# A hybrid decoder trunk on one core: the two parts of a split weight in one shared tile, and the compressed values of both groups in one

## Chip, core and metric

One core of a Trainium2 chip runs the whole program. The metric is device time in microseconds, the median of the runs shown. Engines are named as in the profile: PE (TensorE, matrix products), PEld (its weight loads, which run beside the products), DVE (VectorE), ACT (ScalarE), POOL (GpSimd), SP (SyncE, which issues most transfers).

## What is computed

Two layers of a hybrid decoder over 256 tokens of width 2048. Each layer normalises `x`, applies one wide input projection, feeds its columns to a sparse-attention group and to a Mamba-2 group, and maps the two gated, normalised results back with one output projection:

```python
h = rmsnorm(x, norm_w)
proj = jnp.einsum("bsd,dp->bsp", h, w_in)
(q, kc, vc, ks, vs, kw, vw, gate, z_attn, xbc, dt, z_ssm) = split_columns(proj)
k_cmp = rope(compress_blocks(kc.reshape(kv_shape), pe_k, w1_k, w2_k), pos_cmp)
v_cmp = compress_blocks(vc.reshape(kv_shape), pe_v, w1_v, w2_v)
...
mixed = jnp.concatenate([y_attn, y_ssm], axis=-1)
return x + jnp.einsum("bsm,md->bsd", mixed, w_out)
```

`compress_blocks` makes one compressed key or value for every 16 tokens: chunks of 32 tokens plus a position term, a product with `w1`, SiLU, a product with `w2`. There are two key/value groups.

## The kernel before

**Items.** `ITEMS` (line 55) is a fixed list that one Python loop (line 919) turns into instructions, in an order written out by hand. A "p" item is half a column tile of the input projection, an "o" item a piece of the output projection, a "w" item a piece of the `w1` product. Each layer has 186 p items (93 column tiles, two halves each) and 64 o items. Every p or o item has one weight of 128x1024 floats, loaded by SP into `wr` (five buffers) two to five items ahead.

**Two parts.** To get more precision than one fp32r product gives, each operand is split: `split` (line 154) lets ACT copy the weight into `wh` (the part that fp32r holds) and DVE subtract it from the original into `wl` (the rest). Both have four buffers of 4096 bytes per partition, and both are made two items ahead (`LH = LL = 2`). The other operand is a tile of 512 floats, 256 of one part and 256 of the other.

**A p item** (line 947) has eight pairs: a product of `wh` (stationary, 128 columns) with all 512 columns of the operand tile (moving), and one of `wl` with its first 256 columns. **An o item** (`block`, line 968) has the roles exchanged: 128 columns of the operand tile are stationary, 512 columns of `wh` or `wl` move; 12 products of 512 columns for each item.

**Operand tiles.** In layer 0 the p items move the tiles `h0` to `h15`; the o items of the first half read the Mamba-2 results in `s0` to `s15`, and those of the second half the attention results in `h0` to `h15`. In layer 1 the names are exchanged: p items move `s` tiles, the first half of the o items reads `h`, the second half `s`.

**Addresses.** A tile's place in a partition follows from the order of first allocation and from the sizes, rounded up to 32 bytes; it is software and known before a run. Modulo 256 bytes, the products' operands begin here:

```
                        before
wh, wl (all buffers)    0x80      first ones at 0x19580 and 0x1d580, 4096 bytes apart
h0 to h15               0x80      h0 at 0x21580
s0 to s15               0xc0      s0 at 0x2d6c0
B (att. probabilities)  0x80
V                       0xc0
```

A slice of a tile begins a whole multiple of 512 bytes further, so these numbers hold for every product of a kind.

**Side work.** Small stages are generators in `sides`; `tick` (line 326) advances each by one step at the end of every item, and `W(k)` (line 110) lets a generator rest for `WAITS[k]` items. Each column tile is emptied from PSUM by `evac` (line 341: ACT, DVE), and POOL multiplies it by the norm (`rmul`). For the compression, `build_U` (line 585, three DVE instructions, one call for each of kc 0, kc 1, vc 0, vc 1) adds the position term into `U` after `W(43)`; w items read `U`; `cmp_side` (line 596) applies SiLU into `hd` (line 271, zeroed once at the start by POOL) and the `w2` product. For values (`kv == 1`) eight ACT copies and four DVE subtractions of 32x128 move the result into `VC[0]` and `VC[1]` (lines 629 to 636), which the attention reads at line 796. `v_side` (line 650) transposes a value tile on PE (line 656) into a PSUM tile `t`, of which there are two, copies it with ACT and subtracts with DVE (line 661).

**End of a projection.** In the second half of an output projection DVE adds a finished 128x512 block to `xt`, ACT squares it, and only then come the next copies of `split` in ACT's order (lines 982 to 987).

Of the kernel before, what the change touches and what calls it, by code (L numbers as in the profile page):

```python
# [12 lines left out]
F32R = mybir.dt.float32r  # L13
# [14 lines left out]

NF = 4
WARM = (2, 1, 0, 1, 1, 0, 1, 0)  # L30
WAITS = [1, 0, 0, 4, 0, 2, 0, 0, 0, 2, 0, 2, 0, 0, 0, 1, 1, 2, 0, 0, 0, 1, 1, 0, 3, 3, 2, 2, 0, 2, 1, 1, 2, 1, 0, 1, 1, 1, 1, 4, 3, 1, 1, 3, 4, 0, 1, 0, 0, 4, 4, 2, 2, 0, 1, 2, 0, 2, 2, 0, 1, 1, 1, 3]
EN = 3
ROPE, SINW = 37, 2
W1S, W1N, W1B = 8, 2, 4
# [47 lines left out]
WITEMS = [it for it in ITEMS if it[0] != "w"]  # L82
NS = len(WITEMS)
# [4 lines left out]
def body(ctx: ExitStack, tc: tile.TileContext, wst, w1, xin, xtk, pos, w2, par, con, fin, y):  # L88
    nc = tc.nc
    ACT, DVE, PE, POOL = nc.scalar, nc.vector, nc.tensor, nc.gpsimd  # L90
    HEAD = ((0, 1), (1, 3), (3, 6), (6, 8))
    RS = ((5, 6, 7), (1, 3, 4))
    NR, NH, NL, LH, LL = 5, 4, 4, 2, 2

    pp = ctx.enter_context(tc.tile_pool(name="pp", bufs=1))
    qq = ctx.enter_context(tc.tile_pool(name="qq", bufs=1, space=bass.MemoryType.PSUM))
# [5 lines left out]
    def sb(shape, tag, dt=F32, bufs=1):  # L102
        cnt[0] += 1
        return pp.tile(shape, dt, tag=tag, name=f"{tag}_{cnt[0]}", bufs=bufs)

    def pst(tag, shape=(128, 512), bufs=1):
        cnt[0] += 1
        return qq.tile(list(shape), F32, tag=tag, name=f"p{tag}_{cnt[0]}", bufs=bufs)

    def W(k):  # L110
        for _ in range(WAITS[k]):
            yield
# [3 lines left out]
    def act(out, in_, f=AF.Copy, **kw):  # L116
        if f in (AF.Ln, AF.Exp) and table[0] != AF.Exp:
            ACT.preload_act_table_set("natural_log_exp_and_others")
            table[0] = AF.Exp
        elif f in (AF.Silu, AF.Sin):  # L120
            table[0] = f
        ACT.activation(out, in_, f, **kw)  # L122

    def tt(out, a, b, op):
        DVE.tensor_tensor(out, a, b, op=op)  # L125
# [4 lines left out]
    def f(ap):  # L130
        return ap.bitcast(F32)

    def lo(out, full, hi):
        tt(out, full, f(hi), OP.subtract)

    def mm(out, lhsT, rhs, start, stop):
        PE.matmul(out, lhsT, rhs, start=start, stop=stop, skip_group_check=True)  # L137
# [6 lines left out]
    raw, hi_t, lo_t = {}, {}, {}  # L144
    state = {"dma": 0, "hi": 0, "lo": 0}

    def pump_dma():
        while state["dma"] < min(state["lo"] + NR, DEPTH * NS):
            d = state["dma"]
            raw[d] = sb([128, 1024], "wr", bufs=NR)  # L150
            nc.sync.dma_start(raw[d], wst[d])
            state["dma"] += 1

    def split(i, part=1024):
        while state["hi"] < min(i + LH + 1, DEPTH * NS):
            j = state["hi"]
            state["hi"] += 1
            hi_t[j] = sb([128, 1024], "wh", F32R, bufs=NH)
            for c in range(0, 1024, part):
                act(hi_t[j][:, c:c + part], raw[j][:, c:c + part])  # L160
        while state["lo"] < min(i + LL + 1, DEPTH * NS):
            j = state["lo"]
            state["lo"] += 1
            lo_t[j] = sb([128, 1024], "wl", F32R, bufs=NL)
            for c in range(0, 1024, part):
                lo(lo_t[j][:, c:c + part], raw[j][:, c:c + part], hi_t[j][:, c:c + part])
            pump_dma()
# [23 lines left out]
    state["dma"] = 1  # L191
    for a, b in HEAD:
        c = NK + 384 * a if a else 0
# [70 lines left out]
    onr = one.to_broadcast([128, 128])  # L264

    KT = [sb([128, 2, 2, 272], f"KT{g}", F32R) for g in range(2)]
    VC = [sb([96, 2, 128], f"VC{g}", F32R) for g in range(2)]
    PC = [None]
    for t in KT:
        POOL.memset(f(t[:, :, 0, 256:272]), 0.0)  # L270
    hd = sb([128, 2, 128], "hd")
    POOL.memset(hd, 0.0)
    hg = hd.rearrange("p b (g n) -> p b g n", g=2)
    cs = sb([128, 2, 32], "cs")
    dts = sb([128, 2, 32], "dts")
    gates = sb([128, 2, 48], "gates")
# [75 lines left out]
    def rope(u, c, s):  # L352
        n = u.shape[-1]
        t = sb([128, 256], "rt")
        t = t[:, :n] if len(u.shape) == 2 else t[:, :u.shape[1] * n].rearrange("p (a b) -> p a b", b=n)
        tt(t[0:64], u[64:128], s[64:128], OP.mult)
        tt(t[64:128], u[0:64], s[0:64], OP.mult)
        tt(u, u, c, OP.mult)
        tt(u, u, t, OP.add)
# [7 lines left out]
    h = [None] * NK  # L367

    def make_h(a, b):
        for k in range(a, b):  # L370
            h[k] = sb([128, 512], f"h{k}", F32R)
            scaled(xk[k], nw0[:, k:k + 1], h[k])

    state["hi"] = state["lo"] = 1
    hi_t[0] = sb([128, 1024], "wh", F32R, bufs=NH)
    lo_t[0] = sb([128, 1024], "wl", F32R, bufs=NL)
    w0h, w0l = (t[0].rearrange("p (k c) -> p k c", k=8) for t in (hi_t, lo_t))
    for a, b in HEAD:
        make_h(a, b)
        act(w0h[:, a:b], raw0[:, a:b])  # L380
        lo(w0l[:, a:b], raw0[:, a:b], w0h[:, a:b])
    split(1 - LH, 512)
    nc.sync.dma_start(xt[:, 1], xtk[:, 1])

# [11 lines left out]
    for L in range(DEPTH):  # L396
# [199 lines left out]
        def cmp_side(kv, acc):  # L596
            s = sb([128, 256], "uu", bufs=3)
            act(s, acc[:, :256])
            yield from W(44)
            yield from W(45)  # L600
            ps = pst("t", bufs=2)
            for b in range(2):
                mm(ps[:, b * 32:b * 32 + 32], s[:, b * 128:b * 128 + 128], i4, True, True)
            yield from W(46)
            for c in (0, 48):
                act(hg[:, :, :, c:c + 16], ps[:, 0:64].rearrange("p (b g n) -> p b g n", b=2, g=2), AF.Silu)
            yield from W(47)
            yield from W(48)
            wc = C["w2"][:, 2 * kv:2 * kv + 2]
            ps = pst("t", bufs=2)  # L610
            if kv == 0:
                for b in range(2):
                    mm(ps[:, 0:32], wc[:, b], hg[:, b, :, 0:16], b == 0, b == 1)
                yield from W(49)
                u = C["U", 0][:, 0]
                act(u, ps[:, 0:32].rearrange("p (a b) -> p a b", a=2))
                bc = [t[:, None, 31::16].to_broadcast([128, 2, 15]) for t in (cosT, sinT[0])]
                rope(u[:, :, 0:15], bc[0], bc[1])
                yield from W(50)
                for g in range(2):  # L620
                    act(KT[g][:, 0, 0, 256:271], u[:, g, 0:15])
                    lo(KT[g][:, 1, 0, 256:271], u[:, g, 0:15], KT[g][:, 0, 0, 256:271])
                C["kcmp"] = 1
            else:
                for g in range(2):
                    for b in range(2):
                        mm(ps[0:64, 128 * g:128 * g + 128], hg[:, b, g], wc[:, b], b == 0, b == 1)
                yield from W(51)
                for g in range(2):
                    for t in range(2):  # L630
                        for r in (0, 32):
                            act(VC[g][r:r + 32, t], ps[32 * t:32 * t + 32, 128 * g:128 * g + 128])
                yield from W(52)
                for g in range(2):
                    for t in range(2):
                        lo(VC[g][64:96, t], ps[32 * t:32 * t + 32, 128 * g:128 * g + 128], VC[g][0:32, t])
                C["vcmp"] = 1

        def k_side(u, g, b):
# [39 lines left out]
        def att_side(p, Q):  # L679
            g = p // 4  # L680
# [90 lines left out]
            pcc = PC[0]  # L771
# [6 lines left out]
            for hh in range(2):  # L778
                q = slice(128 * hh, 128 * hh + 128)
# [9 lines left out]
            o = pst("o")  # L789
# [3 lines left out]
                mm3(o, vv[:, 0, 0], vv[:, 0, 1], PH[:, c], PL[:, c], k == 0, False)  # L793
            o2 = o.rearrange("p (h q) -> p h q", h=2)
            for t in range(2):
                mm(o2[:, :, 128 * t:128 * t + 128], VC[g][:, t], pcc.rearrange("p (h q) -> p h q", h=2), False, False)
            o2 = o2[:, :, 128:256]
            for k in range(2):
                vv = V[g][k]
# [5 lines left out]
            a = reg[:, 512 * p:512 * p + 512]  # L805
# [11 lines left out]
            if p == 7:  # L817
                yield
                r = sb([128, 256], "uu", bufs=3)
# [99 lines left out]
        for it in ITEMS:  # L919
            if it[0] == "w":  # L920
                kv, j = it[1], it[2]
# [5 lines left out]
                for m in range(2):  # L927
                    q = 2 * (j % 2) + m
# [12 lines left out]
            if it[0] == "p":  # L941
                if first:
                    acc_of[it[1:3]] = pst("o") if slot == 1 else pst("b1") if slot == 3 else pst("pj", bufs=2)
                ps = acc_of[it[1:3]]
                wh = hi_t[i].rearrange("p (k c) -> p k c", k=8)
                wl = lo_t[i].rearrange("p (k c) -> p k c", k=8)
                n = 2 if L or slot else 1
# [8 lines left out]
                if i < 24:  # L956
                    split(i)
                flush()
                split(i)
            else:  # L960
                cb, kp, half = it[1:]
# [4 lines left out]
                ps = acc_of["o"]  # L966
# [94 lines left out]
        h = nxt  # L1061
# [117 lines left out]
```

## Time and profile before

| | |
|---|---|
| runs | 1593.57, 1593.83, 1594.46 us; median 1593.83 us |
| profiled execution | 1593.89 us, of which the span from first to last instruction 1592.1 us |
| PE busy | 1575.5 us, 99% of the span |
| DVE, ACT, POOL busy | 1215.1, 1057.4, 375.7 us (76%, 66%, 24%) |
| granted TensorE clock | 0.998 of full speed |
| DMA | 302 MB, 190 GB/s mean |

The profile is one execution seen by the hardware profiler, times in microseconds from the start of the span. The page gives busy time and the chain of work that ended last. The trace behind it answers further: groups of equal instructions with their mean duration, the chain in order of time, a timeline of one stretch, and lists of who waited for whom. The duration of a matrix product in the trace (near 395 ns for 512 columns) holds the time that it lies in the pipe; how far apart products start (near 230 ns) is what it costs.

### The profile page before, as it was taken

The page shows a single profiled execution, that of the slowest core. Times are in us where ns is not written, and L with a number is a line of the kernel's source. Part 1 is how long each engine was busy: PE and PEld are TensorE (multiplying, and loading weights), DVE is VectorE, ACT ScalarE, POOL GpSimd, SP SyncE. Part 2 cuts the span into 40 slices and gives each one's busy share as a digit, 9 for nine tenths or more (in the row PEclk, how much of TensorE's full clock was granted, in tenths as well). Part 3 has the DMA queues.
Part 4 walks back from the last instruction along what each step waited for, and adds up shares of the span by engine and source line. Part 5 has one row for each costly group of instructions (what it writes and reads, how often), then busy time and mean ns, then how long its engine had stood idle before and what let it go on. Part 6 is the DMA issues. An engine that isn't in the chain of part 4 may idle for free.

```text
span 1592.1 us, 24872 instructions
## 1 busy us (share of the span) xinstructions
PE 1575.5 (99%) x9039; PEld 1346.9 (85%) x9039; DVE 1215.1 (76%) x2128; ACT 1057.4 (66%) x1922; POOL 375.7 (24%) x308
## 2 busy tenths in 40 slices
PE   9999999999999999999999999999999999999997
PEld 7888888878888888888888888888788888888876
DVE  7888988887778886674568888889867878766654
ACT  7677877755687887543556777777456888765443
POOL 1233334431123231100013334333311323210000
PEclk9999999999999999999999999999999999999999
DMA  9655565677444445555656666567864444455753
GB/s 341 201 179 193 200 208 201 208 262 244 146 149 147 155 146 159 187 181 179 198 172 195 198 206 203 193 196 226 273 222 149 139 154 155 151 171 173 237 166 125
DMA packets 101003, 301.99 MB, mean 190 GB/s; under 512 B 9889, under 2 KB 26721, under 8 KB 100497
## 3 DMA queue, kind: packets, MB, share of 16 engines
q1 hardware_dynamic: 100224, 297.61, 57.2%
q0 software_dynamic: 368, 1.75, 0.3%
q8 instruction: 71, 1.16, 0.3%
q10 hardware_dynamic: 288, 1.05, 0.2%
q14 instruction: 52, 0.42, 0.1%
HBM read 298.21 MB, written 2.16 MB: 189 GB/s over the span
## 4 chain that ended last, share of the span: by engine, by line
PE 93%; ACT 2%; DVE 2%; DMA 1%; issue 1%; SPq 0%; DVEq 0%; ACTq 0%
PE ppj L137 77%; PE po L137 7%; PE pb L137 6%; ACT wh L122 1%; DVE wl L125 1%; DMA wr<-wst 1%; PE pt L137 0%; PE pt L758 0%; PE po L764 0%; PE pt L757 0%; PE pt L514 0%; DVE xT L125 0%; DMA att<-xin 0%; ACT A L122 0%; ACT VC L122 0%
## 5 line engine op out<-in xcount | busy, mean ns | idle before, releaser
L125 DVE TENSOR_TENSOR wl<-wr,wh 128x1024 fp32r<-128x1024 f32 (+1 forms) x500 | 636.4, 1278 | 218.9 <-ACT wh L122 216.4
L122 ACT ACTIVATE wh<-wr 128x1024 fp32r<-128x1024 f32 (+1 forms) x500 | 516.5, 1050 | 90.8 <-PE ppj L137 49.5
L137 PE MATMUL ppj<-h,wh 128*128 128x512 f32 x1456 | 462.8, 399 | 0.7 <-DVE h L128 0.5
L137 PE MATMUL ppj<-s,wh 128*128 128x512 f32 x1456 | 456.2, 395 | 0.0
L137 PEld LDWEIGHTS ppj<-h,wl 128*128 128x128 f32 x1456 | 274.1, 188 | 65.2 <-DVE wl L125 0.6
L137 PEld LDWEIGHTS ppj<-s,wl 128*128 128x128 f32 x1456 | 273.4, 188 | 60.9
L137 PE MATMUL ppj<-h,wl 128*128 128x256 f32 x1456 | 288.0, 279 | 0.0
L137 PE MATMUL ppj<-s,wl 128*128 128x256 f32 x1456 | 287.6, 279 | 0.0
L339 POOL TENSOR_TENSOR uu<-uu,rr 128x256 f32<-128x256 f32 x120 | 146.5, 1222 | 507.9 <-DVE uu L125 501.9
L137 PEld LDWEIGHTS ppj<-h,wh 128*128 128x128 f32 x1456 | 222.5, 189 | 7.2 <-ACT wh L122 4.8
L137 PEld LDWEIGHTS ppj<-s,wh 128*128 128x128 f32 x1456 | 220.6, 188 | 5.0 <-issue 2.2
L122 ACT ACTIVATE ev<-ppj 128x256 f32<-128x256 f32 x182 | 68.9, 379 | 190.0 <-PE ppj L137 180.1
L137 PE MATMUL ppj<-wh,s 128*128 128x512 f32 x384 | 122.3, 396 | 0.0
L137 PE MATMUL ppj<-wh,h 128*128 128x512 f32 x384 | 120.4, 391 | 0.0
L339 POOL TENSOR_TENSOR za<-za,rr 128x256 f32<-128x256 f32 x34 | 41.6, 1223 | 270.5 <-DVE za L125 238.8
L137 PEld LDWEIGHTS ppj<-wh,s 128*128 128x128 f32 x384 | 72.2, 188 | 17.5 <-DVE xT L125 0.2
L137 PEld LDWEIGHTS ppj<-wh,h 128*128 128x128 f32 x384 | 72.1, 188 | 15.5 <-DVE xT L125 0.6
L122 ACT ACTIVATE A<-A,nm 128x128 f32<-128x128 f32 (+2 forms) x192 | 75.4, 394 | 8.7 <-DVE nm L707 8.4
L125 DVE TENSOR_TENSOR uu<-ppj,ev 128x256 f32<-128x256 f32 x116 | 48.6, 419 | 41.1 <-ACT ev L122 41.0
L137 PE MATMUL ppj<-wl,s 128*128 128x512 f32 x192 | 76.0, 396 | 0.1
L137 PE MATMUL ppj<-wl,h 128*128 128x512 f32 x192 | 74.7, 389 | 0.0
L128 DVE SCALAR_TENSOR_TENSOR att<-uu,par,att 128x255 f32<-128x255 f32 (+2 forms) x96 | 60.7, 632 | 2.3
(242 smaller groups left out, 1971.5 us busy)
## 6 DMA issues: line engine op xcount, KB each, us to landing
wr<-wst SPq DMA_DIRECT2D x499, 512.0 KB, 3.6
V<-w SPq DMA_DIRECT2D x64, 256.0 KB, 4.5
B<-cum SPq DMA_DIRECT2D x16, 512.0 KB, 4.7
B<-cum SPq DMA_DIRECT2D x16, 256.0 KB, 6.2
xT<-xtk SPq DMA_DIRECT2D x2, 1024.0 KB, 11.1
att<-fin POOLq DMA_DIRECT2D x1, 1024.0 KB, 8.8
y<-xT SPq DMA_DIRECT2D x4, 256.0 KB, 2.1
y<-xT ACTq DMA_DIRECT2D x2, 512.0 KB, 3.2
```

The source lines that it names most:

```text
L122: ACT.activation(out, in_, f, **kw)
L125: DVE.tensor_tensor(out, a, b, op=op)
L128: DVE.scalar_tensor_tensor(out, a, s, b, op0=op0, op1=op1)
L137: PE.matmul(out, lhsT, rhs, start=start, stop=stop, skip_group_check=True)
L339: POOL.tensor_tensor(dst, dst, rr[0], op=OP.mult)
```

## The change

`wh` and `wl` become the two halves of one tile `wt` of 2048 + 64 floats, four buffers of 8448 bytes; `home(j)` allocates it where `wh` was allocated. For an o item both parts begin `GAP = 16` floats (64 bytes) further in it. `VC` becomes one tile `[96, 2, 2, 128]` with the group as third dimension, so that four ACT copies and two DVE subtractions of 32x256 replace eight and four of 32x128. `hd` is no longer a tile of its own: each layer it is allocated under the tag `SQ` (the attention's sum of squares, used later) inside `cmp_side` and zeroed there by POOL. `SQ` and `nrm` are allocated early, which moves them and what lies behind them. `WAITS[43]` goes from 3 to 2, so `build_U` comes one item sooner.

```diff
+    GAP = 16
-    NR, NH, NL, LH, LL = 5, 4, 4, 2, 2
+    NR, NB, LH, LL = 5, 4, 2, 2
...
+    def home(j):
+        t = sb([128, 2048 + 4 * GAP], "wt", F32R, bufs=NB)
+        a = GAP if WITEMS[j % NS][0] == "o" else 0
+        hi_t[j], lo_t[j] = t[:, a:a + 1024], t[:, a + 1024:a + 2048]
...
-            hi_t[j] = sb([128, 1024], "wh", F32R, bufs=NH)
+            home(j)
...
-            lo_t[j] = sb([128, 1024], "wl", F32R, bufs=NL)
...
-    VC = [sb([96, 2, 128], f"VC{g}", F32R) for g in range(2)]
+    VC = sb([96, 2, 2, 128], "VC", F32R)
...
-    hd = sb([128, 2, 128], "hd")
-    POOL.memset(hd, 0.0)
-    hg = hd.rearrange("p b (g n) -> p b g n", g=2)
+    HD = [None]
+    sb([128, 256], "SQ")
...
+    home(0)
+    for _ in range(2):
+        sb([128, 4], "nrm", bufs=2)
...
+            if kv == 0:
+                hd = sb([128, 2, 128], "SQ")
+                POOL.memset(hd, 0.0)
+                HD[0] = hd.rearrange("p b (g n) -> p b g n", g=2)
+            hg = HD[0]
...
-                for g in range(2):
-                    for t in range(2):
-                        for r in (0, 32):
-                            act(VC[g][r:r + 32, t], ps[32 * t:32 * t + 32, 128 * g:128 * g + 128])
+                for t in range(2):
+                    for r in (0, 32):
+                        act(VC[r:r + 32, t], part_of(t))
...
-                        lo(VC[g][64:96, t], ps[32 * t:32 * t + 32, 128 * g:128 * g + 128], VC[g][0:32, t])
+                for t in range(2):
+                    lo(VC[64:96, t], part_of(t), VC[0:32, t])
...
-                mm(o2[:, :, 128 * t:128 * t + 128], VC[g][:, t], pcc.rearrange("p (h q) -> p h q", h=2), False, False)
+                mm(o2[:, :, 128 * t:128 * t + 128], VC[:, t, g], pcc.rearrange("p (h q) -> p h q", h=2), False, False)
```

The addresses that follow, modulo 256 bytes, worked out from the sizes in the same way:

```
                        before   after
wh, wl of a p item      0x80     0x80    (first buffer at 0x19580, then 8448 bytes apart)
wh, wl of an o item     0x80     0xc0
h0 to h15               0x80     0xc0    (h0 at 0x219c0)
s0 to s15               0xc0     0xc0    (s0 at 0x2dac0)
B, V                    0x80, 0xc0       as before
```

## Rows read from the trace of the kernel before

**Rows 1.** The page: busy us of each engine, share of the span, instructions.
```profile
PE 1575.5 (99%) x9039; PEld 1346.9 (85%) x9039; DVE 1215.1 (76%) x2128; ACT 1057.4 (66%) x1922; POOL 375.7 (24%) x308
```

**Rows 2.** Who waited for whom, PE alone: total us, times, longest us.
```profile
PE pt L656 <- DVE V L125: 2.5, 4, 1.1
PE pb L137 <- DVE B L125: 1.7, 2, 0.9
```

**Rows 3.** Chain in order of time (start us, us, what): two pieces of each layer.
```profile
215.44 16.73 PE ppj L137 x96
...
530.85 11.15 PE ppj L137 x64
...
1004.67 16.59 PE ppj L137 x96
...
1317.20 11.05 PE ppj L137 x64
```

**Rows 4.** Timeline of PE, o items: start us, us, operation; `s` stationary, then `h`.
```profile
690.08 0.63 PE L137 MATMUL ppj<-wh,s 128*128 128x512 f32 x2
...
692.88 0.63 PE L137 MATMUL ppj<-wh,s 128*128 128x512 f32 x2
...
719.91 0.61 PE L137 MATMUL ppj<-wh,h 128*128 128x512 f32 x2
...
722.63 0.61 PE L137 MATMUL ppj<-wh,h 128*128 128x512 f32 x2
```

**Rows 5.** Timeline before the first w item of layer 0, then PE there in both layers.
```profile
319.47 1.65 POOL L339 TENSOR_TENSOR uu<-uu,rr 128x256 f32<-128x256 f32 x1 [1.80 <-DVE uu L125]
...
330.50 0.17 DVE L589 COPY B<-par 128x16 f32<-128x16 f32 x1
...
329.99 0.40 PE L137 MATMUL ppj<-h,wl 128*128 128x256 f32 x2
331.20 1.07 PE L137 MATMUL pb<-V,B 128*32 128x256 f32 x16 [0.82 <-DVE B L125]
...
1118.35 0.40 PE L137 MATMUL ppj<-s,wl 128*128 128x256 f32 x2
1119.64 1.07 PE L137 MATMUL pb<-V,B 128*32 128x256 f32 x16 [0.89 <-DVE B L125]
```

**Rows 6.** Timeline around the compressed values: ACT, DVE, PE in layer 0, PE in layer 1.
```profile
407.76 2.21 ACT L122 ACTIVATE VC<-pt 32x128 fp32r<-32x128 f32 x8
...
409.99 0.38 ACT L122 ACTIVATE ev<-ppj 128x256 f32<-128x256 f32 x1
...
411.36 1.45 DVE L125 TENSOR_TENSOR wl<-wr,wh 128x1024 fp32r<-128x1024 f32 x1 [0.46 <-ACT wh L122]
...
414.59 0.41 PE L656 MATMUL pt<-con,uu 128*128 128x128 f32 x2 [1.06 <-DVE V L125]
...
1201.76 0.41 PE L656 MATMUL pt<-con,uu 128*128 128x128 f32 x2 [1.11 <-DVE V L125]
```

**Rows 7.** Groups by shape (count, busy us, mean ns): ACT's copies from PSUM, two widths.
```profile
L122 ACT ACTIVATE ev<-ppj 128x256 f32<-128x256 f32 x182 | 68.9, 379 | 190.0 <-PE ppj L137 180.1 <-DVE att L128 5.1 <-DVE A L128 2.5
...
L122 ACT ACTIVATE VC<-pt 32x128 fp32r<-32x128 f32 x16 | 4.3, 266 | 0.2
```

**Rows 8.** Timeline: the zeroing at the start, and POOL and ACT where it goes.
```profile
0.86 0.31 POOL L272 MEMSET hd<- 128x256 f32 x1
...
368.33 0.73 POOL L339 TENSOR_TENSOR uu<-uu,rr 128x256 f32<-128x256 f32 x1 [6.28 <-DVE uu L125]
...
372.43 0.34 ACT L122 ACTIVATE hd<-pt 128x64 f32<-128x64 f32 x2 [1.45 <-PE pt L137]
```

**Rows 9.** Waits: ACT's copies into `wh`, whole span; PE for `wl`, 1515 to 1575 us.
```profile
ACT wh L122 <- PE ppj L137: 49.5, 33, 2.8
...
PEld po L137 <- DVE wl L125: 1.2, 2, 0.6
PEld ppj L137 <- DVE wl L125: 0.6, 1, 0.6
```

More of the change, by code (lines that the diff above doesn't have):

```diff
@@ L30 @@
 WARM = (2, 1, 0, 1, 1, 0, 1, 0)
-WAITS = [1, 0, 0, 4, 0, 2, 0, 0, 0, 2, 0, 2, 0, 0, 0, 1, 1, 2, 0, 0, 0, 1, 1, 0, 3, 3, 2, 2, 0, 2, 1, 1, 2, 1, 0, 1, 1, 1, 1, 4, 3, 1, 1, 3, 4, 0, 1, 0, 0, 4, 4, 2, 2, 0, 1, 2, 0, 2, 2, 0, 1, 1, 1, 3]
+WAITS = [1, 0, 0, 4, 0, 2, 0, 0, 0, 2, 0, 2, 0, 0, 0, 1, 1, 2, 0, 0, 0, 1, 1, 0, 3, 3, 2, 2, 0, 2, 1, 1, 2, 1, 0, 1, 1, 1, 1, 4, 3, 1, 1, 2, 4, 0, 1, 0, 0, 4, 4, 2, 2, 0, 1, 2, 0, 2, 2, 0, 1, 1, 1, 3]
 EN = 3
@@ L374, in body @@
     state["hi"] = state["lo"] = 1
-    hi_t[0] = sb([128, 1024], "wh", F32R, bufs=NH)
-    lo_t[0] = sb([128, 1024], "wl", F32R, bufs=NL)
+    home(0)
+    for _ in range(2):
+        sb([128, 4], "nrm", bufs=2)
     w0h, w0l = (t[0].rearrange("p (k c) -> p k c", k=8) for t in (hi_t, lo_t))
@@ L628, in cmp_side, with part_of @@
                 yield from W(51)
-                for g in range(2):
-                    for t in range(2):
-                        for r in (0, 32):
-                            act(VC[g][r:r + 32, t], ps[32 * t:32 * t + 32, 128 * g:128 * g + 128])
+                def part_of(t):
+                    return ps[32 * t:32 * t + 32, 0:256].rearrange("p (g d) -> p g d", g=2)
+                for t in range(2):
+                    for r in (0, 32):
+                        act(VC[r:r + 32, t], part_of(t))
                 yield from W(52)
-                for g in range(2):
-                    for t in range(2):
-                        lo(VC[g][64:96, t], ps[32 * t:32 * t + 32, 128 * g:128 * g + 128], VC[g][0:32, t])
+                for t in range(2):
+                    lo(VC[64:96, t], part_of(t), VC[0:32, t])
                 C["vcmp"] = 1
```

## Prediction

> **What bounds it now.** I read the busy times first: PE is busy 99% of the span, DVE 76% and ACT 66% [rows 1]. Then PE's waits: once the start is over they are few, 2.5 us for the transposes of line 656 and 1.7 us for the first `w1` products [rows 2]. So two things can shorten this kernel: products that start closer together, and those few waits. What DVE, ACT or POOL save elsewhere is worth nothing. The next view is therefore the pace of PE. Equal work does not run at equal pace. Six p items (96 products) take 16.73 us in layer 0 and 16.59 us in layer 1; four take 11.15 and 11.05 us [rows 3]. The instructions are the same; the moving tile is `h` in layer 0 and `s` in layer 1. In the o items, one item of 12 products takes 692.88 - 690.08 = 2.80 us where the stationary operand is an `s` tile and 722.63 - 719.91 = 2.72 us where it is an `h` tile [rows 4]: 233.3 against 226.7 ns from start to start. Time or layer is not the reason, since layer 1 exchanges the names. What does differ is where the tiles begin. Modulo 256 bytes, moving start minus stationary start is 0 in the p items of layer 0 (slower) and 64 in layer 1 (faster); in the o items it is 0 with `h` (faster) and 192 with `s` (slower). I have no rule that gives all four, only the four measured cases.
>
> **Part 1, addresses, p items.** After the change `h` begins at 0xc0 and the p weights stay at 0x80: exactly the starts that layer 1 has now. Layer 0 should take layer 1's pace. The gain per item is (16.73 - 16.59) / 6 = 23 ns or (11.15 - 11.05) / 4 = 25 ns [rows 3], say 24; times 186 items, less two in the slow start, 4.4 us. Layer 1 keeps its difference, 64, and its pace.
>
> **Part 1, addresses, o items.** The weights move to 0xc0, where `h` and `s` now both begin: difference 0 for all, as in today's faster half. The 32 items of each layer with `s` go from 2.80 to 2.72 us, 64 x 0.08 = 5.1 us [rows 4]; those with `h` stay. Here the trace has no exact precedent: it shows difference 0 with both starts at 0x80, none with both at 0xc0. I bound a product by the two levels seen, 226.7 and 233.3 ns, and take the first, because the difference is what it shares with that row. The buffers are now 8448 bytes apart, which is 33 x 256, so the numbers modulo 256 hold for all four; modulo 512 every second one differs, and the trace can't tell whether that counts (a rival below).
>
> Here stands a rule against the change. The Trainium skill, "SBUF — State Buffer", section "Who interferes with whom", gives PE two independent read ports, one for the moving operand and one for weight loads, and says that PE and ACT never wait on anyone. By it a tile's start would be indifferent and part 1 worth nothing; the 2.80 and 2.72 us of equal items speak against it [rows 4].
>
> **Part 2, the shared buffer.** It removes nothing. What it adds: ACT may overwrite a `wh` only when the last `wl` product of its former tenant is done too, at most two 256-column products later, 0.23 us (a pair of products takes 16.73 / 48 = 0.349 us, its third part is 0.116) [rows 3]. ACT waits for PE before such a copy in 33 cases [rows 9], and the weight is needed only two items, 5.6 us, later; behind ACT wait its copies out of PSUM and then DVE's `wl`, both in that slack. An o item ends with a `wh` product, so there nothing is added. I take 0, and 0.5 us as the upper bound for places with little slack.
>
> **Part 3, the values `U` one item sooner.** PE starts the last two 256-column products before the first w item at 329.99 us, so the next could start at 330.22; it starts at 331.20, held by DVE's `B` [rows 5]. That is 0.98 us; in layer 1, 1118.58 against 1119.64, 1.06 us [rows 5]. DVE builds that `U` at 330.50, though its input has been finished by POOL near 321 [rows 5]. One item sooner is some 2.8 us, which puts the end of the build near 329, ahead of PE. Queued behind the moved build on DVE is one `wl` subtraction, about 1.2 us later but for a weight two items ahead; ACT and POOL get no new wait. Gain 2.0 us, bounds 1.0 (if DVE's queue only lets half of it through) and 2.0. The calls for vc move as well; no wait of PE hangs on those [rows 2]. Late next there is nothing: the weights of the following item are made.
>
> **Part 4, compressed values.** PE's wait at 414.59 us (1.06 us), and the same in layer 1 (1.11 us), is for DVE's `V` at line 661 [rows 6]. Followed back: DVE's `wl` at 411.36 waited for ACT's `wh`, that followed `ev` at 409.99, which followed eight `VC` copies that took 2.21 us [rows 6]. Four copies of 256 columns cost about 0.38 us each, by the 256-column copy from PSUM (379 ns), in place of eight at 0.27 [rows 7]: 1.52 us, 0.7 us less. All of it reaches PE, as the wait is longer than that: 1.4 us for two layers; bounds 0 (if another DVE wait is right behind) and 2.2 (the whole wait). The two DVE subtractions saved come after this point and save nothing on PE.
>
> **Part 5, zeroing.** POOL's memset of 0.31 us [rows 8] goes, in each layer, behind the `rmul` that ends at 369.06 and ahead of ACT's SiLU, which starts at 372.43 because it waits for PE anyway [rows 8]: 3 us of cover, cost 0. Without the cover ACT would start 0.3 us later. The `SQ` buffer is free of other use then.
>
> **What is given back.** At the ends of the last projection PE waits three times, about 0.6 us, for a `wl` that hangs on ACT and DVE after a finished block [rows 9]. PE reaches these points sooner by 0.08 us an item, one to two items after the block; each wait grows by some 0.13 us: 0.4 us lost.
>
> **Sum.** 4.4 + 5.1 + 2.0 + 1.4 - 0.4 = 12.5 us off the profiled execution's 1593.89 us (span 1592.1 and 1.8 outside it), which stands 0.06 us from the median of the runs: 1581.4 us.
>
> **Rivals.** (a) *The start does not count*: the pace follows from something else that goes with the tiles. Then only parts 3 and 4 remain: 1593.9 - 3.4 = 1590.5. (It is also what the rule of the Trainium skill's page "SBUF — State Buffer", quoted above, would give.) For it: no mechanism is shown. Against: all four cases follow the tiles and not the time. (b) *In o items the stationary tile's own start counts, not the difference*: 0xc0 is the slower one. Then all o items run at 2.80 us, +5.1 in place of -5.1: 1593.9 - 4.4 + 5.1 - 3.4 = 1591.2. For it: rows 4 fit this as well. (c) *The relation repeats every 512 bytes*: every second weight buffer stands wrong. Half of the p items of layer 0 gain 2.2, half of layer 1's lose 2.2; half of the o items with `s` gain 2.6 and half of those with `h` lose 2.6: only 3.4 us remains, 1590.5. (d) *The unseen case is a worse level*, the slower rival: in the o items with both starts at 0xc0, one more step of 6.7 ns, 240 ns. The products with `h` lose 13.3 ns, those with `s` 6.7 ns, 768 of each: +15.3 us against 7.8 saved: 1601.4. It decides from a mean of 235 ns on (7.8 us over 1536 products above today's mean of 230). For it only that the case is unseen.
>
> **How the numbers follow.** Forecast 0.82, (a) 0.04, (b) 0.06, (c) 0.04, (d) 0.04. The predicted time is 1581.4 us. Its own range is worked out from the bounds: at the upper end part 3 gives 1.0 less, part 4 1.4 less, part 2 takes 0.5 and a quarter of part 1's o gain is lost to phases after stalls (1.3): 1585.6, say 1586; at the lower end part 4 gives 0.8 more, nothing is given back (0.4) and 1 us is left for rounding in the pace: 1579. With (a) to (d) outside, that leaves out little under 2 in 10. This kernel's measurement tells 0.2% (3.2 us) from no change: faster below 1590.6, slower above 1597.0. Faster has the forecast and half of (a) and (c), which lie on the border: 0.86; within 0.2% the rest of these and (b), 0.10; slower (d), 0.04.
>
> **What would show it.** In the profile after: pieces of 96 products of p items near 16.59 us in both layers; o items at 2.72 us with `h` and `s` alike. No wait of PE for `B` before the w items, and a wait for `V` of about 0.4 us. Wrong would be: o items at 2.80 us everywhere (b), a pace that alternates with the buffer (c), p items of layer 0 at 16.73 us (a), or a new entry of PE waiting for DVE's part of `wt` (part 2).

## Result and profile after

The changed kernel takes 1584.61 us (median of 4 runs, 1583.64 to 1584.93), beside 1593.70 us for the kernel before in the same session (1593.23 to 1594.46): the medians differ by 9.1 us, and the ratio of the runs is 0.9941 with a 95% interval of 0.9924 to 0.9959. The profiled execution of the changed kernel took 1584.93 us with a span of 1583.2 us. The median lies inside the range of the forecast (1579 to 1586 us), 3.2 us above its 1581.4 us. What has to be explained is 12.5 us forecast against 9.1 us found (8.9 us between the two profiled executions).

Of the page, the busy line, to be set beside [rows 1]. PE is down by 7.8 us of busy time with the same 9039 instructions; DVE and ACT have lost 4 and 8 instructions, and 1.2 and 0.6 us.

```profile
PE 1567.7 (99%) x9039; PEld 1347.5 (85%) x9039; DVE 1213.9 (77%) x2124; ACT 1056.8 (67%) x1914; POOL 374.3 (24%) x309
```

PE's waits in the changed kernel (total us, times, longest), to be set beside [rows 2]:

```profile
PE pt L666 <- DVE V L126: 2.1, 4, 0.8
PE pb L138 <- DVE za L366: 1.5, 1, 1.5
PE ppj L138 <- ACT wt L123: 0.9, 1, 0.9
PE po L138 <- DVE wt L126: 0.8, 2, 0.4
...
PE po L138 <- DMA V<-w: 0.4, 1, 0.4
PE ppj L138 <- DVE wt L126: 0.3, 1, 0.3
```

The waits for `B` are gone. The waits for `V` have fallen from 2.5 only to 2.1 us; where 0.4 us was forecast, 0.8 us is left in each layer. PE now shows three waits for DVE's part of `wt`, where it had one of 0.2 us, and one for a transfer of `w1`. The prediction named an entry for `wt` as a sign against the shared buffer (part 2); the first experiment below decides that.

The chain's pieces (start, us, what), to be set beside [rows 3]: layer 0, layer 0, layer 1, layer 1. Both layers now have the pace that only layer 1 had.

```profile
214.64 16.59 PE ppj L138 x96
...
526.34 11.05 PE ppj L138 x64
...
997.65 16.59 PE ppj L138 x96
...
1309.93 11.05 PE ppj L138 x64
```

The groups of o products by form (count, busy us, mean ns of one) show the same for the o items; a product's own length is more than its distance to the next, since products overlap. `s` and `h` are now alike; the items of [rows 4] differed by 0.08 us.

```profile
L138 PE MATMUL ppj<-wt,s 128*128 128x512 f32 x576 | 133.0, 391 | 0.3 <-DVE wt L126 0.3
L138 PE MATMUL ppj<-wt,h 128*128 128x512 f32 x576 | 132.9, 390 | 0.0
```

The timeline before the first w item, to be set beside [rows 5]: DVE's build of `U`, PE's first w products in layer 0, and those in layer 1. `U` is finished at 326.98 + 1.08 = 328.06 us, 0.6 us before PE comes, and neither row of PE has a wait behind it.

```profile
326.98 1.08 DVE L126 TENSOR_TENSOR B<-uu,par 128x256 f32<-128x256 f32 x2
...
328.67 1.07 PE L138 MATMUL pb<-V,B 128*32 128x256 f32 x16
...
1111.68 1.07 PE L138 MATMUL pb<-V,B 128*32 128x256 f32 x16
```

The timeline around the compressed values, to be set beside [rows 6]. The four copies take 1.52 us, as forecast. But `ev` behind them now has a wait that it did not have: 0.43 us for PE, which ends that column tile only then. From there on the chain is the old one.

```profile
404.35 1.52 ACT L123 ACTIVATE VC<-pt 32x256 fp32r<-32x256 f32 x4
...
406.30 0.39 ACT L123 ACTIVATE ev<-ppj 128x256 f32<-128x256 f32 x1 [0.43 <-PE ppj L138]
...
406.79 0.42 DVE L126 TENSOR_TENSOR uu<-ppj,ev 128x256 f32<-128x256 f32 x1 [3.16 <-ACT ev L123]
...
407.66 1.45 DVE L126 TENSOR_TENSOR wt<-wr,wt 128x1024 fp32r<-128x1024 f32 x1 [0.45 <-ACT wt L123]
...
410.33 0.41 DVE L126 TENSOR_TENSOR V<-pt,V 128x256 fp32r<-128x256 f32 x1
...
410.89 0.41 PE L666 MATMUL pt<-con,uu 128*128 128x128 f32 x2 [0.82 <-DVE V L126]
...
1194.48 0.41 PE L666 MATMUL pt<-con,uu 128*128 128x128 f32 x2 [0.82 <-DVE V L126]
```

**Where the 8.9 us between the two profiled executions come from.** Both programs issue PE's products in nearly the same order, so the distance from each product's start to the next can be set beside its counterpart and the differences summed by kind (us):

```
                                              forecast    found
p items with h, layer 0                         -4.4      -4.13
o items with s, both layers                     -5.1      -4.56
o items with h, p items with s                   0         0.0
waits for B (U one item sooner)                 -2.0      -1.85
waits for V (compressed values)                 -1.4      -0.52
given back: last projection 0.61, other
  o blocks 0.19, s products at 208 us 0.40      +0.4      +1.20
w products, transfers of w1                       -       +0.45
start, up to 31 us                                -       +0.30
rest                                              0       +0.19
sum                                            -12.5      -8.92
```

A distance at the border of two kinds can be counted to either, which moves single rows by some 0.1 us.

Two of the given-back places. In the last projection stand all three waits of PE for DVE's `wt` in the list above (0.8 us in two, 0.3 in one). The waits of PE's loads at the same three places, to be set beside the last two lines of [rows 9], show that each is 0.2 us longer than before, where 0.13 had been forecast:

```profile
PEld po L138 <- DVE wt L126: 1.6, 2, 0.8
PEld ppj L138 <- DVE wt L126: 0.8, 1, 0.8
```

At 208 us PE reaches the products of `s` with `one` before POOL has made the `s`; POOL and PE's load in the timeline of the changed kernel:

```profile
206.84 0.74 POOL L571 TENSOR_TENSOR s<-att,s 128x256 fp32r<-128x256 f32 x1 [0.53 <-ACT s L123]
...
207.63 0.18 PEld L138 LDWEIGHTS pt<-s,one 128*128 128x128 f32 x1 [0.34 <-POOL s L571]
```

### The profile page after: what moved, and what is told of

Same layout as the page of the kernel before. It is cut to its first block, busy times and chain, and to the rows that moved or that the text cites. A ratio compares the mean times of both kernels' runs of the same rounds, so it can differ in the third digit from the quotient of the medians.

```text
span 1583.2 us, 24861 instructions
## 1 busy us (share of the span) xinstructions
PE 1567.7 (99%) x9039; PEld 1347.5 (85%) x9039; DVE 1213.9 (77%) x2124; ACT 1056.8 (67%) x1914; POOL 374.3 (24%) x309
## 4 chain that ended last, share of the span: by engine, by line
PE 91%; DVE 3%; ACT 2%; issue 2%; POOL 1%; DMA 1%; SPq 0%; DVEq 0%; POOLq 0%; ACTq 0%
PE ppj L138 75%; PE po L138 7%; PE pb L138 6%; DVE wt L126 1%; ACT wt L123 1%; PE pt L138 1%; PE pt L768 0%; DVE att L129 0%; PE po L774 0%; PE pt L767 0%; PE pt L519 0%; DVE xT L126 0%; DMA att<-xin 0%; DMA V<-w 0%; POOL Q L510 0%
## 5 line engine op out<-in xcount | busy, mean ns | idle before, releaser
L126 DVE TENSOR_TENSOR wt<-wr,wt 128x1024 fp32r<-128x1024 f32 (+1 forms) x500 | 638.4, 1281 | 216.6 <-ACT wt L123 215.4
L123 ACT ACTIVATE wt<-wr 128x1024 fp32r<-128x1024 f32 (+1 forms) x500 | 516.9, 1051 | 88.8 <-PE ppj L138 49.4
L138 PE MATMUL ppj<-h,wt 128*128 128x512 f32 (+1 forms) x2912 | 521.9, 338 | 1.4 <-ACT wt L123 0.9
L138 PE MATMUL ppj<-s,wt 128*128 128x512 f32 (+1 forms) x2912 | 518.1, 337 | 0.0
L138 PEld LDWEIGHTS ppj<-h,wt 128*128 128x128 f32 x2912 | 449.6, 189 | 69.3 <-ACT wt L123 4.2
L138 PEld LDWEIGHTS ppj<-s,wt 128*128 128x128 f32 x2912 | 447.3, 188 | 65.9 <-issue 2.6
L138 PE MATMUL ppj<-wt,s 128*128 128x512 f32 x576 | 133.0, 391 | 0.3 <-DVE wt L126 0.3
L138 PE MATMUL ppj<-wt,h 128*128 128x512 f32 x576 | 132.9, 390 | 0.0
L138 PEld LDWEIGHTS ppj<-wt,s 128*128 128x128 f32 x576 | 107.4, 188 | 23.5 <-DVE wt L126 0.8
L138 PEld LDWEIGHTS ppj<-wt,h 128*128 128x128 f32 x576 | 107.4, 188 | 22.8 <-DVE xT L126 0.7
```

## Experiments

### One number back: the start of the o weights

```
-        a = GAP if WITEMS[j % NS][0] == "o" else 0
+        a = 0
```

> The changed kernel with one number undone: the o weights start at 0x80 modulo 256 in the shared buffer, as the p weights do, so that moving minus stationary start is 192 for all o items; buffers, U and the compressed values stay as changed. Theory (the difference of the starts sets the pace of a product): every o item, with h and with s, takes 2.80 us in place of 2.73, about 128 x 0.071 = 9.1 us more than the changed kernel: 1593.7 us; the p items keep 2.765 us. Rival (the pace comes from the shared buffer or from something else that the change moved, not from the start): o items stay at 2.73 us and the time within 1 us of 1584.6.

Measured: 1592.91 us (ratio to before 0.9991, 0.9982 to 1.0001), so 8.3 us above the changed kernel's 1584.61 us, from 64 bytes; 9.1 us had been expected. In the trace all four kinds of o products are 5.8 to 6.25 ns further apart than in the changed kernel, 9.2 us in all; the p items are unchanged. The groups of this kernel:

```profile
L138 PE MATMUL ppj<-wt,s 128*128 128x512 f32 x576 | 136.2, 396 | 0.1
L138 PE MATMUL ppj<-wt,h 128*128 128x512 f32 x576 | 136.2, 396 | 0.0
```

Buffer, order and names are those of the changed kernel, so the start alone makes this difference, and rival (a) of the prediction falls. The waits at the three places of the last projection are 0.2 us shorter each again, 0.6 us in all, which is why the time grew by less than 9.2 us: they were given back because PE came sooner, not because of the shared buffer. Past the start (43 us), PE and its loads wait no longer for a weight in this kernel than in the kernel before, so the shared buffer itself costs nothing that shows.

### U one item later again

```
-WAITS = [..., 2, 4, 0, 1, ...]      # entry 43
+WAITS = [..., 3, 4, 0, 1, ...]
```

> The changed kernel with U built one item later again (entry 43 of WAITS is 3, as before). Theory (part 3 is worth what the two waits showed): PE waits again for B before the first w item in both layers, 0.8 and 0.9 us in the list of waits, and the time is 1.9 us more than the changed kernel's, 1586.5 us. Rival (the step could be taken by any slack behind it): the waits return, but the time grows by less than 0.5 us, because the transposes of line 666 or the wait for the transfer of w1 behind it shrink by as much.

Measured: 1585.77 us (ratio to before 0.9948, 0.9934 to 0.9963). Both waits are back, and PE's distances at these two places grow by 0.96 us each, 1.92 us. The time grew by 1.2 us where 1.9 had been expected. That is no more than the medians of one kernel differ between two sessions (1584.61 and 1585.78 us for the changed kernel, below), so the trace decides and not the time. In the trace the start is 0.5 us shorter in this execution, and the transfers of `w1`, of which more below, cost 0.5 us less. No other wait of PE shrank in return. PE in layer 0 and in layer 1:

```profile
329.18 1.07 PE L138 MATMUL pb<-V,B 128*32 128x256 f32 x16 [0.89 <-DVE B L126]
...
1113.06 1.07 PE L138 MATMUL pb<-V,B 128*32 128x256 f32 x16 [0.89 <-DVE B L126]
```

### Eight copies of compressed values

```
-                for t in range(2):
-                    for r in (0, 32):
-                        act(VC[r:r + 32, t], part_of(t))
+                for g in range(2):
+                    for t in range(2):
+                        for r in (0, 32):
+                            act(VC[r:r + 32, t, g], part_of(t)[:, g])
```

(the subtractions in the same way)

> The changed kernel with eight copies of 128 columns (and four subtractions) into the one tile of compressed values, as before, in place of four of 256 columns. Theory of the prediction: the copies take 0.7 us longer and PE's wait for V at line 666's transposes grows by all of it, by 0.7 us in each layer, 1.4 us in all. Rival (what the trace of the changed kernel suggests): the copy of ev behind them could not have started earlier anyway, since PE ends that column tile only then, so the wait grows by 0.2 to 0.3 us in each layer, 0.5 us in all.

A second trace of the same kernel:

> The changed kernel with eight copies of compressed values, once more, for a second trace; its first had no wait for the transfer of w1, though its timing up to there is that of the changed kernel. Theory (the landing varies): this trace may have such a wait, unlike the first; PE's waits for V at 410 and 1193 us are again 0.29 us longer than the changed kernel's. Rival (the wait depends on the program): no wait for V<-w again.

Measured: PE's wait for `V` grows by 0.29 us in each layer, 0.57 us in all, in both executions. The rival's number holds, not the prediction's 1.4 us. ACT and PE in layer 0, PE in layer 1:

```profile
404.50 2.21 ACT L123 ACTIVATE VC<-pt 32x128 fp32r<-32x128 f32 x8
...
406.74 0.39 ACT L123 ACTIVATE ev<-ppj 128x256 f32<-128x256 f32 x1
...
411.33 0.41 PE L668 MATMUL pt<-con,uu 128*128 128x128 f32 x2 [1.11 <-DVE V L126]
...
1194.14 0.41 PE L668 MATMUL pt<-con,uu 128*128 128x128 f32 x2 [1.11 <-DVE V L126]
```

With eight copies `ev` follows at once and shows no wait; with four it shows 0.43 us of waiting. 0.7 us saved less 0.43 of new wait leaves some 0.27; 0.29 reached PE. The two executions took 1584.47 and 1586.14 us (one run each), and their PE distances differ by 1.7 us in all: 1.4 us of it in the w products. The first lost 1.2 us to late transfers there, the second 2.6; PE's loads at one group of w items of the second:

```profile
1148.96 0.14 PEld L138 LDWEIGHTS po<-V,A 128*32 128x32 f32 x4 [0.52 <-DMA V<-w]
1149.65 0.14 PEld L138 LDWEIGHTS po<-V,A 128*32 128x32 f32 x4 [0.55 <-DMA V<-w]
```

### The transfer of w1: the same two kernels again

> The changed kernel once more, unaltered, for a second trace and for a median from more runs beside the next kernel. Theory (PE's wait of 0.4 us for the transfer of w1 at 1163 us in the first trace hangs on when that transfer happens to land): the wait is shorter or gone, or stands at another w item, and the median lies between 1583.5 and 1585 us. Rival (it belongs to the changed timing): the same wait stands at the same w item, about 1 us with what follows it.

> The kernel before, unaltered, for a second trace. The changed kernel's two traces have a wait of PE for the transfer of w1 (0.4 us at 1163 us, 0.8 at 1164), the first trace of before has none, though issue and use of that transfer are 6.07 us apart in both. Theory (the landing varies by some tenths of a us from execution to execution): waits for V<-w appear in this trace too, at this or another w item. Rival (the changed timing makes that transfer late): none here.

Measured: the changed kernel 1585.78 us (1584.85 to 1586.54, ratio to before 0.9946, 0.9932 to 0.9960); before 1594.39 us (one run). The median of the changed kernel is above the 1583.5 to 1585 us that had been expected. In its second trace the wait stands at the same place and is longer. The first trace, SP's issue of the four transfers and PE; then the second:

```profile
1155.44 3.11 SPq L412 DMA_DIRECT2D V<-w  x4
...
1161.51 1.06 PE L138 MATMUL po<-V,A 128*32 128x256 f32 x12
...
1163.01 0.62 PE L138 MATMUL po<-V,A 128*32 128x256 f32 x4 [0.44 <-DMA V<-w]
```

```profile
1156.18 3.08 SPq L412 DMA_DIRECT2D V<-w  x4
...
1162.25 1.06 PE L138 MATMUL po<-V,A 128*32 128x256 f32 x12
...
1164.15 0.62 PE L138 MATMUL po<-V,A 128*32 128x256 f32 x4 [0.85 <-DMA V<-w]
```

From issue to use there are 1161.51 - 1155.44 = 6.07 us, and 6.07 us at the counterpart in the kernel before. That is the first of the four transfers, though, and the late products are the last four, which read the fourth. The fourth one's issue in the changed kernel, then in the kernel before, and the products that it serves there:

```profile
1158.16 0.38 SPq L412 DMA_DIRECT2D V<-w  x1
...
1164.89 1.51 SPq L407 DMA_DIRECT2D V<-w  x1
...
1169.59 1.07 PE L137 MATMUL po<-V,A 128*32 128x256 f32 x16
```

Where nothing is late, the fourth transfer's first product starts 0.67 us after the first of the 16. So its issue begins 4.0 us ahead of use in both traces of the changed kernel, against 5.4 and 4.7 us in the two of the kernel before: in the changed kernel SP's second issue of the four took 1.7 us in both traces in place of some 0.35, in the kernel before it was the fourth (1.5 us) or the third (1.1 us). From the start of its issue to its landing the fourth took 4.8 and 5.2 us in the changed kernel, 4.8 and 3.8 in the one before. What makes one of the issues long no run shows.

The w items come in 16 groups of four, with 16 products each. To see the lateness whole I took, for each group, the time from its first product's start to its last one's; where nothing is late it is 0.691 us. What lies above that, summed (us):

```
before                 1.48   again 0.73
changed                1.93   again 3.09
o weights at 0x80      2.41
U one item later       1.41
eight copies           1.20   again 2.57
V one item sooner      1.77   again 1.26     (below)
```

Of one kernel the two executions differ by 0.5 to 1.4 us, and every trace has some of it. So a good part is a matter of the execution. Neither expectation holds whole: the kernel before has such lateness too, but at the group of 1163 us both traces of the changed kernel are late and both of before are not. Of the eight traces of kernels with the shared buffer in the list, six are late there, all but the two with eight copies. On the whole these eight lost 2.0 us on average (1.2 to 3.1), the two of before 1.1. So the rival, that the changed timing adds a little here, is neither shown nor excluded.

Taken without it, and without the first 200 products, the changed kernel's two executions are 9.4 and 9.9 us shorter than those of before: 1529.4 and 1529.3 us against 1538.8 and 1539.2.

### A map of starts

```
-        a = GAP if WITEMS[j % NS][0] == "o" else 0
+        it, n = WITEMS[j % NS], j % NS
+        a = 4 * ((n // 6) % 16) if it[0] == "p" else 4 * (it[1] + 4 * it[3] + 8 * (j // NS))
```

> The changed kernel with the weights' start in the shared buffer varied: o items in 16 blocks of 8, each with an own start, 0, 16, ... 240 bytes beyond 0x80; p items in groups of 6, in turn with the same 16 starts. The pace of the products in each group gives pace against difference of starts. Theory (the difference modulo 256 bytes sets it): 226.7 ns an o product where the difference is 0 and 233.3 where it is 192, and of p pairs 345.0 where it is 64 and 348.6 where it is 0, in whichever layer and place the group stands; between them steps or a slope that no run has shown, and where the best start is. Rival (the pace goes with a tile, a layer or a place): the groups of one layer or tile have one pace whatever their start.

The finer ones, with the starts of the other differences in the same place of the code:

> The changed kernel with starts varied in steps of 4 bytes: o items in 16 blocks with differences 28, 24, ... -32; p items in groups of 6 with the first part at the same 16 differences and the second at 64, 60, ... 4. It shows where between the 16-byte steps the pace turns. Theory (the difference of starts of what is moved and what is loaded): 226.8 ns again at difference 0 of the o items, 228.2 again at 32 and 229.5 at 64 of the 512-column products, 115.5 at 0 of the 256-column ones, each whatever the other part's start; what lies between is not known. Rival (the two parts act on each other): the values at 32, 64 and 0 do not return, because the other part stands elsewhere than in the first map.

> The changed kernel with both parts of a weight again at one start, as in the first map, but at the differences that the first map left out: p items in groups of 4 at the 48 differences modulo 256 that are multiples of 4 and not of 16, o items in groups of 3 at those between 36 and 220. It looks for a start that beats both kernels. Theory (64 and 0 are the best there are; the pace is set by how the two streams meet, and differences that are no multiple of 16 have nothing that those lack): no p group under 2.76 us an item and no o group under 2.72 us. Rival (the steps of 16 bytes missed a better one): a p group at some 2.74 us an item or less, worth 0.02 x 184 = 4 us and more.

Measured: 1602.75, 1603.60 and 1607.56 us (one run each), all above both kernels. The mean distance of products of equal shape, from all starts in the trace without stalls, by difference of moving and stationary start modulo 256 bytes: an o product, and a p pair (512 and then 256 columns), ns:

```
difference    0    16    32    48    64    80    96   112   128   144   160   176   192   208   224   240
o product  226.8 231.7 233.4 233.3 231.0 231.1 233.3 231.0 233.3 233.3 234.2 233.4 233.3 234.7 233.3 236.4
p pair     348.8 351.5 346.9 350.0 345.7 349.6 353.0 351.6 349.1 351.6 351.5 350.5 347.3 346.7 351.1 353.3

multiples of 4 between (36 to 220 for o, all for p): o 228.1 (60) to 240.0 (116); p 346.9 (228) to 358.9 (52)
o nearest to 0: 252 229.0, 4 237.2, 248 232.1, 8 233.3;   28 227.7
```

(The table counts moving minus stationary start; by that the o items of the finer map run from -28 to 32, the reverse of what is written above.) The levels known from before return: 226.8 and 233.3 for o at 0 and 192, 348.8 and 345.7 for p at 0 and 64. The p groups at 0 and at 64 have these levels in both layers, so there the pace goes with the difference and not with tile or layer. In the maps each difference of the o items stands in few places; that their pace goes with the difference, the changed kernel (0 for both tiles in both layers) and the first experiment (192 for all) show. But it is no smooth function: 4 bytes beside 0 an o product takes 237.2 ns. For the o products the remainder modulo 16 bytes orders much of it: 233.6 to 239.9 ns where the difference is 4 above a multiple of 16 (mean 237.2), 227.8 to 232.7 where it is 12 above (mean 229.9), and means near 233 at 0 and 8. Of the 64 differences that are multiples of 4, with both parts of a weight at one start, 0 is the best for o and 64 the best for p, and these are the two that the changed kernel has; in these executions no better one lay between. The difference does not determine all: at 240 the first map has 236.4 ns and the finer one 233.2.

### Two parts of a weight at two starts

```
-        a = GAP if WITEMS[j % NS][0] == "o" else 0
-        hi_t[j], lo_t[j] = t[:, a:a + 1024], t[:, a + 1024:a + 2048]
+        b, a = (16, 1040) if WITEMS[j % NS][0] == "o" else (8, 1040)
+        hi_t[j], lo_t[j] = t[:, a:a + 1024], t[:, b:b + 1024]
```

> The changed kernel with the two parts of a p weight at two starts: the first part at 0xc0 modulo 256 (difference 0 to the moving tile), the second at 0xa0 (difference 32); o items as changed. In the map of 16 starts the 512-column product was shortest at difference 32 (228.2 ns; 229.5 at 64) and the 256-column product at difference 0 (115.5 ns; 116.2 at 64). During a 512-column product the second part is loaded for the next one, during a 256-column product a first part. Theory (what counts is the tile that is loaded while a product moves, each product by its own difference): a pair takes 228.2 + 115.5 = 343.7 ns in place of 345.5, 1.8 ns over some 2940 pairs, 5.3 us less than the changed kernel, 1579.3 us. Rival (the tile that is multiplied with counts, not the one being loaded): the 512-column products then stand at difference 0 (233.2 ns) and the 256-column ones at 32 (118.7): 351.9 ns a pair and 1603 us.

Measured: 1595.70 us (ratio to before 1.0015, 1.0005 to 1.0025), 11 us slower than the changed kernel. The p items lose in both layers; the pieces of 96 and 64 products, of layer 0 twice and of layer 1:

```profile
215.90 16.79 PE ppj L138 x96
...
530.28 11.20 PE ppj L138 x64
...
858.40 16.79 PE ppj L138 x96
```

Both accounts fall. A pair takes 350.0 ns on average: neither 343.7 (the tile being loaded counts) nor 351.9 (the tile being multiplied counts). My working had a slip: products of a kind come in twos (the `x2` of [rows 5]), so only every second load is of the other part. With that the first account gives (233.2 + 228.2) / 2 + (118.7 + 115.5) / 2 = 347.8 ns, still not what was measured. The finer map says the same: the values at 64, 32 and 0 did not return where the other part stood elsewhere (512 columns, second part at 32 and first at 252: 233.1 ns in place of 228.2). Neither way of pricing the products one by one holds; how the two parts act together is open.

### V one item sooner

```
-WAITS = [..., 2, 2, 0, 1, 1, 1, 3]      # entry 58
+WAITS = [..., 2, 1, 0, 1, 1, 1, 3]
```

> The changed kernel with the copies and subtractions into V one item sooner (entry 58 of WAITS is 1, not 2). It tests what part 4 left: PE's wait of 0.8 us in each layer for V's subtraction, which stands on DVE behind the weight's subtraction and the row maxima. Theory (that place in DVE's queue is the next limit, and DVE is idle for 3 us one item sooner): the waits of line 666 for V, 2.1 us in all, fall to under 0.3 us and the time by 1.8 us, to 1582.8 us. Rival (the transposes are late by their own pt buffers, or V's subtraction one item sooner only waits for PE there): the waits stay or move, and the time stays within 0.5 us of 1584.6.

> The kernel with V one item sooner, once more, on the same chip as the changed kernel. Theory: PE has none of the waits of line 666 for V, 0.38 and 0.98 us in each layer, 2.7 us in all, and the median lies 2.7 us below that of the changed kernel. Rival (1582.0 us came from a good start of those runs): within 1 us of it.

Measured: 1582.00 us (1580.21 to 1583.01, ratio to before 0.9923, 0.9909 to 0.9938), and again, beside the changed kernel's 1585.78 us on one chip, 1582.26 us (1580.38 to 1582.87, ratio to before 0.9922, 0.9910 to 0.9935): 3.5 us below it and 12.6 below before. This version beats both kernels. All four waits of line 666 are gone, 0.37 and 0.98 us in each layer, 2.7 us; the lateness of `w1` was 1.8 us less in that trace and its first 200 products took 0.8 us more. The same stretch as above in this kernel: `V` is made at 405.45 on ACT and 405.87 on DVE, ahead of `ev`, in the 3.16 us that DVE stood idle there in the changed kernel, and PE's transposes at 409.75 us wait for nothing.

```profile
403.91 1.52 ACT L123 ACTIVATE VC<-pt 32x256 fp32r<-32x256 f32 x4
405.45 0.39 ACT L123 ACTIVATE V<-pt 128x256 fp32r<-128x256 f32 x1
405.87 0.42 DVE L126 TENSOR_TENSOR V<-pt,V 128x256 fp32r<-128x256 f32 x1 [2.73 <-ACT V L123]
406.14 0.38 ACT L123 ACTIVATE ev<-ppj 128x256 f32<-128x256 f32 x1 [0.30 <-PE ppj L138]
...
409.75 0.38 PE L666 MATMUL pt<-con,uu 128*128 128x128 f32 x2
```

## Why the prediction was right, and where it was off

**Part 1, p items: right.** 4.13 us of 4.4. Layer 0 took over layer 1's pace, and the map shows the same two levels in both layers.

**Part 1, o items: right.** 4.56 us of 5.1; the unseen case, both starts at 0xc0, ran at the level of both at 0x80. The term was 0.5 too large because 0.08 us an item came from two rounded rows; the mean over all products is 6.0 ns each, 0.071 us an item. (b) falls by the o items of the changed kernel, (c) because the o products have one pace in all four buffers of the changed kernel (227.0 to 227.5 ns) and the p pairs too (345.4 to 345.8), (d) by the same pace, against 240 ns, (a) by the single number put back. The Trainium skill ("SBUF — State Buffer", "Who interferes with whom"), by whose two read ports and a PE that waits on nobody a start would be indifferent, does not agree: 64 bytes were worth 9.2 us of PE's distances here, and the measurement decides.

**Part 2: right, 0.** With the o weights' start put back and the shared buffer kept, PE's waits for weights past the start are those of the kernel before. The entry for `wt`, which the prediction would have read as a sign against this part, came from PE's earlier arrival.

**Part 3: right.** 1.85 us of 2.0, and 1.92 when undone.

**Part 4: the step that failed.** "All of it reaches PE, as the wait is longer than that." The copies did become 0.7 us shorter, but the chain back from PE's wait had a second input, `ev`'s own: PE's end of the column tile, ready some 0.27 us before the copies were through. Only that much could be gained in a layer: 0.52 us for both found where 1.4 was summed, inside the bounds of 0 to 2.2. The row of `ev` shows no wait in [rows 6] because ACT was the later of the two; how much earlier the other one was is not in that row, and I did not read it off PE's.

**Part 5: right, 0.** POOL's zeroing in the changed kernel and ACT's SiLU into the same tile, in layer 0 (4.2 us of cover; in layer 1 it is 3.8):

```profile
365.91 0.32 POOL L612 MEMSET SQ<- 128x256 f32 x1
...
370.46 0.34 ACT L123 ACTIVATE SQ<-pt 128x64 f32<-128x64 f32 x2
```

**Given back: too small.** 1.20 us against 0.4. The mechanism held in the last projection (0.61 us at three places, forecast 0.4). Forgotten were the other o blocks (0.19) and any place in the p items: by 208 us PE is earlier, and POOL's `s` is late by 0.40.

**Not in the sum.** The lateness of `w1`'s transfers (1.93 - 1.48 = 0.45 us between the two profiled executions) and the start (0.30). Both vary from one execution to the next by more than that; whether the change adds to the first is open.

Together: part 4 0.88, given back 0.80, o items 0.54, `w1` 0.45, start 0.30, p items 0.27, part 3 0.15 and a rest of 0.19 make the 3.6 us between 12.5 and 8.92.

## What to carry to other kernels

Where equal products run at unequal pace, compare the starts of the tiles that PE reads: here a shift of 64 bytes was worth 8 us of 1590, and only a relation that some part of the kernel already shows should be counted on. When a step ahead of a wait is shortened, read at each link of the chain back how early its other input was ready; the smallest of these, not the length of the wait, bounds the gain. When PE gets faster on the whole, look for every place where another engine was only just in time, and take something off for each.

## What the runs showed of the hardware

The distance between 512-column products with a load beside each ran from 226.8 to 240.0 ns over the 64 differences of starts that are multiples of 4 bytes, and that of a p pair from 345.7 to 358.9 ns. Neither is a slope: 4 bytes can make 10 ns, and the one order seen is the o products' by the remainder modulo 16 (4 slow, 12 fast). What in the memory or in PE does this no run shows; with the two parts of a weight at two starts, neither way tried of pricing each product by its own difference gave the 350.0 ns a pair that were measured. The fourth of the four transfers of `w1` before the last group took 3.7 to 5.2 us from the start of its issue to its landing in the ten executions listed. PE lost 0.7 to 3.1 us to late ones in an execution, while two executions of one kernel, taken without that and without their start, agreed within 0.5 us.
